# A channel-major residual stream, out and down projections with stationary weights, and weight parts in three slots at equal residues

## The chip, the cores and the metric

The kernel runs on one core of a Trainium2 chip. TensorE (PE) multiplies, VectorE (DVE) and ScalarE (ACT) work element by element, GpSimd (POOL) does a few small things, and SyncE (SP) issues the transfers of the weights. The metric is the device time of one execution in microseconds.

## The reference

One layer of a hybrid decoder on 256 tokens of 2048 channels, in float32. It needs these products, by far the largest part of the work:

```python
h = rmsnorm(x, g_mix);  proj = h @ w_in             # 2048 x 5200
x = x + concat([pool_out, attn_out]) @ w_out        # 2048 x 2048
u = rmsnorm(x, g_ffn) @ w_up                        # 2048 x 11264
uc = causal_conv3(u); gate, val = split(uc)
x = x + (silu(gate) * val) @ w_down                 # 5632 x 2048
x = x + (p @ w_ple_proj) * sigmoid(rmsnorm(x, g_ple) @ w_ple_gate)
return rmsnorm(x, g_final)
```

Between the first two lines stand trailing-mean pooling and a sparse attention whose indexer picks 64 keys for each query. The change does not touch either.

## The kernel before

**Products.** Every float32 operand is cut into a high part `hi` that TensorE takes in one pass (type float32r) and a low rest `lo`. A product is hi·hi + hi·lo + lo·hi. One *block* here is a 128x128 piece of a weight matrix, applied to all 256 tokens: 768 columns stream through the array for it, in one of two forms.

- `cm_matmul` (lines 121 to 127; "cm" for channel-major): the weight block is stationary. Line 125 streams the activations' hi and lo, 512 columns, past `hi`. Line 126 streams the activations' hi, 256 columns, past `lo`. A block is two matmuls and two weight loads, and the output has channels in the partitions.
- `tm_matmul` (lines 143 to 153; "tm" for token-major): a 128x128 tile of activations is stationary and 512 columns of weights stream past it. Lines 150, 151 and 152 are the three terms; four blocks take six matmuls of 512 columns. The output has tokens in the partitions.

Before the change w_qi, w_qk, w_u (together 512 blocks) and w_up (1408 blocks) are cm; w_first, w_out (256 blocks), w_down (704 blocks), w_pp and w_pg are tm.

**Units.** `unit` (lines 59 to 68) brings in 8 blocks of weights at a time: a DMA on SP's queue into one of four `raw` buffers, ACT copies it to `hi` (line 65), DVE subtracts to make `lo` (line 67). `hi` and `lo` come from two pools, `whi` and `wlo`, of three buffers each, 4416 bytes a buffer and partition, one behind the other. Units take these three slots in turn. In the built program slot s has `hi` at byte 91904 + 4416 s of each partition and `lo` at 105152 + 4416 s. The activations `hT`, 16 tiles of 2048 bytes (256 tokens hi, 256 tokens lo), stand at byte 36064; block i of a unit is 512 bytes further in the slot than block i - 1, and its tile of `hT` 2048 bytes further than the last.

**Residual.** `x` holds the stream with tokens in the partitions. `add_residual` (lines 169 to 174) adds 512 output columns of w_out or w_down to it and squares them on ACT. `to_hT` (lines 155 to 167) then transposes those four channel tiles on TensorE (line 162, eight transposes for 512 columns), and `split` writes hi and lo into `hT`. `rstd_col` and `rstd_rows` make the inverse root mean square as a column for each token and, with two small matmuls (line 117), as a row `rbc`. The first stage loads both x transposed (`xr`) and x itself.

**Order.** The instructions' order on each engine is set by a scheduler that simulates a timeline; each engine runs its queue strictly in order.

Of the kernel before, what the change touches and what calls it, by code (L numbers as in the profile page):

```python
# [10 lines left out]
F32 = mybir.dt.float32  # L11
# [24 lines left out]


# [7 lines left out]
def layer(ctx: ExitStack, tc: tile.TileContext, a: dict):  # L45
# [4 lines left out]
    cst = ctx.enter_context(tc.tile_pool(name="cst", bufs=1))  # L50
    wraw = ctx.enter_context(tc.tile_pool(name="wraw", bufs=4))
    whi = ctx.enter_context(tc.tile_pool(name="whi", bufs=3))
    wlo = ctx.enter_context(tc.tile_pool(name="wlo", bufs=3))
# [4 lines left out]

    def unit(src, n=1024, keep=None):

        size, bufs = (1024, 8) if keep else (UNIT, None)
# [3 lines left out]
        A.copy(hi[:, :n], raw[:, :n])  # L65
        lo = (keep or wlo).tile([P, size], F32R, name="lo", bufs=bufs)
        V.tensor_sub(lo[:, :n], raw[:, :n], hi[:, :n].bitcast(F32))  # L67
        return hi, lo
# [6 lines left out]
    x = cst.tile([P, 2, D], F32, name="x")  # L75
    hT = cst.tile([P, KT, 2 * S], F32R, name="hT")
    rbc = cst.tile([P, S], F32, name="rbc")
    mhalf = cst.tile([P, 2], F32, name="mhalf")
    G.memset(mhalf, -0.5)
    NU = 4  # L80
# [40 lines left out]
    def cm_matmul(ps, hi, lo, kts, first, last):  # L121

        for i, kt in enumerate(kts):
            w = slice(i * P, (i + 1) * P)
            T.matmul(ps, hi[:, w], hT[:, kt, :], start=first and i == 0, stop=False)  # L125
            T.matmul(ps[:, :S], lo[:, w], hT[:, kt, :S],  # L126
                     start=False, stop=last and i == len(kts) - 1)

    def cm_tile(src, c, ps=None):
        if ps is None:  # L130
            ps = acc.tile([P, 512], F32, name="pa")
        for h in range(2):
            hi, lo = unit(src[c][:, h * 1024:(h + 1) * 1024])
            cm_matmul(ps, hi, lo, range(8 * h, 8 * h + 8), h == 0, h == 1)
        return ps

    def cm_evict(dst, ps):
        b = tmp.tile([P, S], F32, name="eb", bufs=3)
# [16 lines left out]
    def to_hT(n, gcol):  # L155

        for kp in range(2):
            ps = aux.tile([P, 512], F32, name="ps")
            for j in range(2):
                kt = 4 * n + 2 * kp + j  # L160
                for t in range(2):
                    T.transpose(ps[:, j * S + t * P:j * S + (t + 1) * P],  # L162
                                x[:, t, kt * P:(kt + 1) * P], ident)
            for j in range(2):
                kt = 4 * n + 2 * kp + j
                split(hT[:, kt, :S], hT[:, kt, S:], ps[:, j * S:(j + 1) * S],
                      prm[:, gcol + kt:gcol + kt + 1])

    def add_residual(n, pss, ssq):
        for t in range(2):  # L170
            xs = x[:, t, n * 512:(n + 1) * 512]
            V.tensor_add(xs, pss[t], xs)
            sq = tmp.tile([P, 512], F32, name="sq")
            A.activation(sq, xs, AF.Square, accum_out=ssq[:, t, n:n + 1])

    def sum4(ssq):
        s = tmp.tile([P, 2], F32, name="s4")
        V.tensor_reduce(s, ssq, axis=AX.X, op=OP.add)
        return s

    ssq_f = cst.tile([P, 2, 4], F32, name="ssq_f")
    ssq_p = cst.tile([P, 2, 4], F32, name="ssq_p")


    with ExitStack() as c1:
        ar = c1.enter_context(tc.tile_pool(name="ar", bufs=1))
        catP = ar.tile([P, 8, 2 * S], F32R, name="catP")


        xr = [ar.tile([P, 8, S], F32, name="xr0", tag="tb"),  # L190
# [536 lines left out]
```

## Time and profile before

| | |
|---|---|
| device time, median of 3 (lowest, highest) | 1210.94 us (1210.93, 1210.98) |
| device time of the profiled execution | 1210.77 us |
| its span in the profile | 1209.0 us |
| PE busy | 1197.5 us, 99% |
| DVE, ACT busy | 817.0 us, 68%; 625.4 us, 52% |
| granted TensorE clock | 0.997 over the span |

[...] A float32 matmul that is not a transpose stands as two records, and a transpose or a float32r matmul as one.

### The profile page before, as it was taken

To read this page: it belongs to the slowest core of one execution; us is meant where nothing else is said; L and a number is where in the kernel's file an instruction comes from. 1 tells how busy PE (TensorE), PEld (TensorE's weight loads), DVE (VectorE), ACT (ScalarE), POOL (GpSimd) and SP (SyncE) were. 2 spreads that over 40 slices of the span, in tenths; PEclk is the share of its full clock that TensorE was granted. 3 is DMA by queue.
4 is the path that set the end of the run, shared out by engine and by line. 5 is a ranking of instruction groups with operands and counts; after the bars stand their busy time and mean duration, and the time that the engine had idled before them with its cause. 6 is when DMAs were issued, how large, how long until landed. Compare 5 with 4: busy or idle time off the path is not lost.

```text
span 1209.0 us, 16727 instructions
## 1 busy us (share of the span) xinstructions
PE 1197.5 (99%) x6332; PEld 1027.2 (85%) x6332; DVE 817.0 (68%) x1234; ACT 625.4 (52%) x951; POOL 8.5 (1%) x26
## 2 busy tenths in 40 slices
PE   9999999999999999999999999999999999999996
PEld 9988888888888888888888888888888888888886
DVE  6566866985557778777777877877545454545565
ACT  7455344555456555555555555555434343434453
POOL 0000000000000000000000000000000000000000
PEclk9999999999999999999999999999999999999998
DMA  9654665456665555555555555556666666666662
GB/s 359 221 184 158 231 201 179 141 161 187 187 186 180 189 190 191 190 188 191 188 188 191 189 193 189 188 191 186 190 190 187 187 183 190 185 187 220 189 213 85
DMA packets 66720, 230.46 MB, mean 191 GB/s; under 512 B 7792, under 2 KB 9464, under 8 KB 66512
## 3 DMA queue, kind: packets, MB, share of 16 engines
q1 hardware_dynamic: 63488, 223.88, 58.5%
q10 hardware_dynamic: 2144, 2.88, 0.7%
q0 software_dynamic: 1008, 2.64, 0.6%
q8 instruction: 49, 0.80, 0.3%
q14 instruction: 31, 0.25, 0.1%
HBM read 226.74 MB, written 3.68 MB: 191 GB/s over the span
## 4 chain that ended last, share of the span: by engine, by line
PE 98%; ACT 0%; DMA 0%; DVE 0%; SPq 0%; issue 0%; POOLq 0%; ACTq 0%
PE pa L125 36%; PE pa L126 19%; PE pa L152 12%; PE pa L151 12%; PE pa L150 12%; PE ps L151 1%; PE ps L152 1%; PE ps L150 1%; PE ps L162 1%; PE ps L290 1%; PE ps L467 0%; DMA raw<-in_w_first 0%; PE ps L377 0%; PE ps L291 0%; PE ps L125 0%; PE ps L428 0%
## 5 line engine op out<-in xcount | busy, mean ns | idle before, releaser
L67 DVE TENSOR_TENSOR lo<-raw,hi 128x1024 fp32r<-128x1024 f32 (+2 forms) x417 | 508.9, 1221 | 350.0 <-ACT hi L65 347.5
L65 ACT CAST hi<-raw 128x1024 fp32r<-128x1024 f32 (+2 forms) x417 | 435.9, 1046 | 534.3 <-issue 218.3
L125 PE MATMUL pa<-hT,hi 128*128 128x512 f32 x1904 | 665.8, 393 | 0.2 <-ACT hi L65 0.2
L126 PE MATMUL pa<-hT,lo 128*128 128x256 f32 x1904 | 534.6, 281 | 0.0
L125 PEld LDWEIGHTS pa<-hT,hi 128*128 128x128 f32 x1904 | 357.7, 188 | 81.4 <-issue 0.6
L126 PEld LDWEIGHTS pa<-hT,lo 128*128 128x128 f32 x1904 | 358.2, 188 | 0.2
L152 PE MATMUL pa<-hi,aT 128*128 128x512 f32 x352 | 138.5, 394 | 0.0
L151 PE MATMUL pa<-lo,aT 128*128 128x512 f32 x352 | 138.5, 393 | 0.0
L150 PE MATMUL pa<-hi,aT 128*128 128x512 f32 x352 | 126.0, 395 | 0.0
L151 PEld LDWEIGHTS pa<-lo,aT 128*128 128x128 f32 x352 | 66.1, 188 | 15.6
L152 PEld LDWEIGHTS pa<-hi,aT 128*128 128x128 f32 x352 | 66.1, 188 | 15.1
L150 PEld LDWEIGHTS pa<-hi,aT 128*128 128x128 f32 x352 | 66.1, 188 | 14.9
L151 PE MATMUL pa<-lo,hT 128*128 128x512 f32 (+2 forms) x208 | 74.8, 360 | 0.1
L152 PE MATMUL pa<-hi,hT 128*128 128x512 f32 (+2 forms) x208 | 74.8, 360 | 0.0
L150 PE MATMUL pa<-hi,hT 128*128 128x512 f32 (+2 forms) x208 | 65.1, 363 | 0.0
L534 ACT ACTIVATE cv<-ub,cnv 128x256 f32<-128x256 f32 x88 | 52.6, 598 | 1.1 <-DVE ub L141 1.0
L140 DVE TENSOR_TENSOR eb<-pa,eb 128x256 f32<-128x256 f32 x119 | 49.8, 418 | 0.0
L538 DVE SCALAR_TENSOR_TENSOR cv<-ub,cnv,cv 128x256 f32<-128x256 f32 x88 | 42.7, 485 | 3.0
L151 PEld LDWEIGHTS pa<-lo,hT 128*128 128x128 f32 x208 | 39.4, 190 | 5.4 <-DVE lo L67 0.4
L152 PEld LDWEIGHTS pa<-hi,hT 128*128 128x128 f32 x208 | 39.4, 189 | 4.9
L150 PEld LDWEIGHTS pa<-hi,hT 128*128 128x128 f32 x208 | 38.7, 191 | 5.7 <-ACT hi L65 0.5
L139 ACT COPY eb<-pa 128x256 f32<-128x256 f32 x119 | 43.5, 365 | 0.0
(174 smaller groups left out, 826.7 us busy)
## 6 DMA issues: line engine op xcount, KB each, us to landing
raw<-in_w_up SPq DMA_DIRECT2D x176, 512.0 KB, 4.7
raw<-in_w_down SPq DMA_DIRECT2D x88, 512.0 KB, 3.6
raw<-in_w_qk SPq DMA_DIRECT2D x32, 512.0 KB, 4.4
raw<-in_w_out SPq DMA_DIRECT2D x32, 512.0 KB, 3.7
raw<-in_w_pg SPq DMA_DIRECT2D x32, 512.0 KB, 4.4
raw<-in_w_first SPq DMA_DIRECT2D x15, 552.0 KB, 6.3
raw<-in_w_qi SPq DMA_DIRECT2D x16, 512.0 KB, 4.2
raw<-in_w_u SPq DMA_DIRECT2D x16, 512.0 KB, 4.2
```

The source lines that it names most:

```text
L65: A.copy(hi[:, :n], raw[:, :n])
L67: V.tensor_sub(lo[:, :n], raw[:, :n], hi[:, :n].bitcast(F32))
L125: T.matmul(ps, hi[:, w], hT[:, kt, :], start=first and i == 0, stop=False)
L126: T.matmul(ps[:, :S], lo[:, w], hT[:, kt, :S], start=False, stop=last and i == len(kts) - 1)
L139: A.copy(b, ps[:, S:])
L140: V.tensor_add(b, ps[:, :S], b)
L150: T.matmul(pss[t][:, :n], xh, hi[:, w], start=first and i == 0, stop=False)
L151: T.matmul(pss[t][:, :n], xh, lo[:, w], start=False, stop=False)
L152: T.matmul(pss[t][:, :n], xl, hi[:, w], start=False, stop=last and i == len(kts) - 1)
L162: T.transpose(ps[:, j * S + t * P:j * S + (t + 1) * P], x[:, t, kt * P:(kt + 1) * P], ident)
L534: A.activation(t, u[:, 2:], AF.Identity, bias=cnv[:, k + 3:k + 4], scale=cnv[:, k + 2:k + 3])
L538: V.scalar_tensor_tensor(t, u[:, :S], cnv[:, k:k + 1], t, op0=OP.mult, op1=OP.add)
```

## The change

`x` is replaced by `xt`, with channels in the partitions. w_out and w_down are stored by block and go through `cm_matmul`, one output tile of 128 channels at a time, w_out in pairs of tiles (`out_unit`). The new `add_residual` adds both halves of the PSUM tile on DVE, splits straight into `hT`, and after every second tile squares the pair on ACT and adds it to `ssa` on DVE. `rstd_tok` sums the squares over the channels with four float32 matmuls of two columns. The transposes move to the end: `to_rows` turns 512 channels of `xt` back to tokens for the last stage, while w_pg runs. The first stage no longer loads x, and w_qi's first tile moves ahead of `rstd_rows`.

The weights' `hi` and `lo` of a unit now share one tile `w` in one of three one-buffer pools `w0`, `w1`, `w2`. In the built program slot s is at byte 73760 + 12288 s, `lo` stands 5056 bytes behind `hi` (4416 in the wider units of the first stage). `hT` stays at 36064, and `catP` (130272), `catA` (146656) and `aT` (134368) get its residue 3296 modulo 4096.

```diff
+LOW, SLOT = 1264, 2304
+GAP_W, GAP_A, GAP_F = 144, 8, 176
...
+    gap.tile([P, GAP_W], F32, name="gap")
+    for i in range(3):
+        wsp.append(ctx.enter_context(tc.tile_pool(name=f"w{i}", bufs=1)))
+        mid.append(ctx.enter_context(tc.tile_pool(name=f"mid{i}", bufs=1)) if i < 2 else None)
+    rbc = mid[0].tile([P, S], F32, name="rbc")
+    ssa = mid[0].tile([P, 2 * S], F32, name="ssa")
...
-        hi = (keep or whi).tile([P, size], F32R, name="hi", bufs=bufs)
-        lo = (keep or wlo).tile([P, size], F32R, name="lo", bufs=bufs)
+            w = wsp[n_units % 3].tile([P, SLOT], F32R, name="w")
+            n_units += 1
+            l0 = LOW if n <= 1024 else UNIT
+            hi, lo = w[:, :n], w[:, l0:l0 + n]
...
-    x = cst.tile([P, 2, D], F32, name="x")
+    xt = cst.tile([P, KT, S], F32, name="xt")
...
+    def add_residual(c, ps, gcol):
+        xs = xt[:, c, :]
+        V.tensor_add(xs, ps[:, :S], xs)
+        V.tensor_add(xs, ps[:, S:], xs)
+        split(hT[:, c, :S], hT[:, c, S:], xs, prm[:, gcol + c:gcol + c + 1])
+        if c % 2:
+            square(c // 2)
...
+            A.activation(sq, pair, AF.Square)
+            V.tensor_add(ssa, ssa, sq)
...
+    def rstd_tok(name):
+        ps = aux.tile([P, 512], F32, name="ps")
+        for t in range(2):
+            for h in range(2):
+                T.matmul(ps[:, 2 * t:2 * t + 2], ssa[:, h * S + t * P:h * S + (t + 1) * P], ones2,
+                         start=h == 0, stop=h == 1)
+        return rstd_col(ps[:, 0:4:2], name)
...
-                in_order(nc.sync.dma_start(x[:, :, cs], a["x"][:, :, cs]))
...
+        for c0 in range(0, KT, 2):
+            ps2 = [acc.tile([P, 512], F32, name="pa") for _ in range(2)]
+            for h in range(2):
+                for e in range(2):
+                    out_unit(c0 + e, ps2[e], h)
+                    if c0 + h + e == 0:
+                        pool_map(*done.pop())
+            for e in range(2):
+                add_residual(c0 + e, ps2[e], C_GFFN)
...
+        for c in range(KT):
+            ps = acc.tile([P, 512], F32, name="pa")
+            for k0 in range(0, NF, 8):
+                k1 = min(k0 + 8, NF)
+                hi, lo = unit(a["w_down"][c][:, k0 * P:k1 * P], (k1 - k0) * P)
+                cm_matmul(ps, hi, lo, tiles(aT, range(k0, k1)), k0 == 0, k1 == NF)
+            add_residual(c, ps, C_GPLE)
...
+        def to_rows(n):
+            for t in range(2):
+                ps = aux.tile([P, 512], F32, name="ps")
+                for j in range(4):
+                    T.transpose(ps[:, j * P:(j + 1) * P], xt[:, 4 * n + j, t * P:(t + 1) * P],
+                                ident)
+                A.copy(gx[:, t, n * 512:(n + 1) * 512], ps)
```

In the changed kernel `cm_matmul` is on lines 145 and 146, `unit`'s two halves on 85 and 86, the ones matmuls on 200, `rstd_rows` on 137 and the last transposes on 604.

PE before, where 512 columns of w_out end and the next begin (`catP` are activations, `ident` the identity, x the residual):

```order
L150 MATMUL pa<-hi,catP 128x512
L151 MATMUL pa<-lo,catP 128x512
L152 MATMUL pa<-hi,catP 128x512
L162 MATMUL ps<-ident,x 128x128 x2
L150 MATMUL pa<-hi,catP 128x512
L162 MATMUL ps<-ident,x 128x128 x6
L151 MATMUL pa<-lo,catP 128x512
L152 MATMUL pa<-hi,catP 128x512
```

PE in the changed kernel, inside w_out, where one unit ends on `catA` and the next begins on `catP`:

```order
L145 MATMUL pa<-catA,w 128x512
L146 MATMUL pa<-catA,w 128x256
L145 MATMUL pa<-catA,w 128x512
L146 MATMUL pa<-catA,w 128x256
L145 MATMUL pa<-catP,w 128x512
L146 MATMUL pa<-catP,w 128x256
L145 MATMUL pa<-catP,w 128x512
L146 MATMUL pa<-catP,w 128x256
```

The six 512-column matmuls of four blocks have become four pairs of 512 and 256 columns, and nothing stands between one output tile and the next.

PE before, at the end of the first stage (`r_mix` is the first inverse root mean square, `hT` the activations):

```order
L150 MATMUL ps<-hi,hT 128x368
L151 MATMUL ps<-lo,hT 128x368
L152 MATMUL ps<-hi,hT 128x368
L117 MATMUL ps<-ident,r_mix 128x128 x2
L125 MATMUL ps<-hT,hi 128x512
L126 MATMUL ps<-hT,lo 128x256
```

PE in the changed kernel, at the same place, from the end of w_qi's first unit to the end of its second; between the two pieces stand 12 more of the matmuls of lines 145 and 146:

```order
L145 MATMUL ps<-hT,w 128x512
L146 MATMUL ps<-hT,w 128x256
L200 MATMUL ps<-ones_101,ssa 128x2 x4
L145 MATMUL ps<-hT,w 128x512
L146 MATMUL ps<-hT,w 128x256
...
L145 MATMUL ps<-hT,w 128x512
L146 MATMUL ps<-hT,w 128x256
L137 MATMUL ps<-ident,r_mix 128x128 x2
L145 MATMUL pa<-hT,w 128x512
L146 MATMUL pa<-hT,w 128x256
```

The four ones matmuls are new, and the two of `rstd_rows` now come one unit behind them instead of long behind the sums.

DVE in the changed kernel between the same two places (`ms` is the mean square, w the weights' low part):

```order
L86 TENSOR_TENSOR w<-raw,w 128x1024 x3
L120 TENSOR_SCALAR ms<-ps 128x2
L86 TENSOR_TENSOR w<-raw,w 128x1024
L128 TENSOR_TENSOR r_602<-r_600 128x2
L129 SCALAR_TENSOR_TENSOR r_602<-r_602,ms 128x2
L131 SCALAR_TENSOR_TENSOR r_mix<-r_602,r_600 128x2
```

DVE before, with the same chain in the middle of the first stage:

```order
L178 TENSOR_REDUCE s_568<-ssq_102 128x2
L100 TENSOR_SCALAR ms<-s_568 128x2
L108 TENSOR_TENSOR r_574<-r_572 128x2
L109 SCALAR_TENSOR_TENSOR r_574<-r_574,ms 128x2
L67 TENSOR_TENSOR lo<-raw,hi 128x1104
L111 SCALAR_TENSOR_TENSOR r_mix<-r_574,r_572 128x2
```

The chain from the mean square to `r_mix` has a subtraction of weights inside it in both, and its first link now waits for TensorE.

## Rows read from the trace of the kernel before

**Rows 1.** The page: busy time of each engine, and the chain that ended last.

```profile
PE 1197.5 (99%) x6332; PEld 1027.2 (85%) x6332; DVE 817.0 (68%) x1234; ACT 625.4 (52%) x951; POOL 8.5 (1%) x26
...
PE 98%; ACT 0%; DMA 0%; DVE 0%; SPq 0%; issue 0%; POOLq 0%; ACTq 0%
```

**Rows 2.** The waits of PE, all of them: waiter, releaser, us, times, longest.

```profile
PE ps L207 <- POOL rbc L82: 1.1, 1, 1.1
PE pa L125 <- ACT hi L65: 0.2, 1, 0.2
```

**Rows 3.** Timeline, PE, w_up: the first matmul of five units running (start, us, line).

```profile
405.37 0.39 PE L125 MATMUL pa<-hT,hi 128*128 128x512 f32 x1
...
408.12 0.40 PE L125 MATMUL pa<-hT,hi 128*128 128x512 f32 x1
...
410.90 0.40 PE L125 MATMUL pa<-hT,hi 128*128 128x512 f32 x1
...
413.72 0.39 PE L125 MATMUL pa<-hT,hi 128*128 128x512 f32 x1
...
416.47 0.40 PE L125 MATMUL pa<-hT,hi 128*128 128x512 f32 x1
```

**Rows 4.** Stretches: busy us (x count) of PE, PEld, DVE, ACT, POOL; clock, DMA share, GB/s.

```profile
0.00:50.00 50.00, 48.79 (x267) 47.30 (x268) 28.00 (x38) 31.97 (x52) 1.54 (x9) 1.00 0.87 316
384.00:848.00 464.00, 464.00 (x2670) 407.50 (x2669) 370.46 (x589) 265.92 (x420) 0.00 (x0) 1.00 0.59 190
918.00:978.00 60.00, 60.00 (x261) 48.72 (x260) 28.93 (x28) 25.26 (x29) 0.00 (x0) 1.00 0.64 187
1121.00:1142.00 21.00, 21.00 (x92) 17.00 (x91) 12.76 (x14) 11.83 (x15) 0.00 (x0) 1.00 0.59 182
```

**Rows 5.** Timeline, PE, w_down: from one group of transposes to the next.

```profile
916.39 0.38 PE L162 MATMUL ps<-ident,x 128*128 128x128 f32 x2
...
916.84 0.82 PE L162 MATMUL ps<-ident,x 128*128 128x128 f32 x6
917.41 0.48 PE L151 MATMUL pa<-lo,aT 128*128 128x512 f32 x1
917.73 0.39 PE L152 MATMUL pa<-hi,aT 128*128 128x512 f32 x1
917.96 0.39 PE L150 MATMUL pa<-hi,aT 128*128 128x512 f32 x1
...
978.10 0.39 PE L152 MATMUL pa<-hi,aT 128*128 128x512 f32 x1
```

**Rows 6.** Timeline, PE: small float32 matmuls (two records each) and the matmul behind.

```profile
79.16 0.49 PE L290 MATMUL ps<-kx,qx 64*128 64x128 f32 x2
79.57 0.39 PE L291 MATMUL ps<-kr,qr 128*128 128x256 f32 x1
...
369.10 0.60 PE L117 MATMUL ps<-ident,r_ffn 128*128 128x128 f32 x4
369.46 0.36 PE L126 MATMUL pa<-hT,lo 128*128 128x256 f32 x1
369.66 0.40 PE L125 MATMUL pa<-hT,hi 128*128 128x512 f32 x1
```

**Rows 7.** Timeline: links of the chain to `r_mix`, and a unit's ACT and DVE work.

```profile
36.52 0.17 DVE L100 TENSOR_SCALAR ms<-s 128x2 f32<-128x2 f32 x1
36.84 0.70 POOL L106 TENSOR_TENSOR r<-ms,mhalf 128x2 f32<-128x2 f32 x1 [35.47 <-DVE ms L100]
37.57 0.16 DVE L108 TENSOR_TENSOR r<-r 128x2 f32<-128x2 f32 x1 [0.88 <-POOL r L106]
...
49.07 1.05 ACT L65 CAST hi<-raw 128x1024 fp32r<-128x1024 f32 x1 [1.89 <-PE ps L152]
50.15 1.23 DVE L67 TENSOR_TENSOR lo<-raw,hi 128x1024 fp32r<-128x1024 f32 x1 [1.63 <-ACT hi L65]
```

**Rows 8.** The page, costliest groups: DVE's 256-column sum out of PSUM (busy, mean ns).

```profile
L140 DVE TENSOR_TENSOR eb<-pa,eb 128x256 f32<-128x256 f32 x119 | 49.8, 418 | 0.0
```

More of the change, by code (lines that the diff above doesn't have):

```diff
@@ L119, in rstd_rows, with cm_matmul, tiles, cm_tile @@
         V.tensor_copy(rbc, ps[:, :S])
-    def cm_matmul(ps, hi, lo, kts, first, last):
-        for i, kt in enumerate(kts):
+    def cm_matmul(ps, hi, lo, acts, first, last):
+        for i, act in enumerate(acts):
             w = slice(i * P, (i + 1) * P)
[L125 to L131, printed above, removed]
+            T.matmul(ps, hi[:, w], act, start=first and i == 0, stop=False)
+            T.matmul(ps[:, :S], lo[:, w], act[:, :S],
+                     start=False, stop=last and i == len(acts) - 1)
+    def tiles(act, kts):
+        return [act[:, kt, :] for kt in kts]
+    def cm_tile(src, c):
+        ps = acc.tile([P, 512], F32, name="pa")
         for h in range(2):
             hi, lo = unit(src[c][:, h * 1024:(h + 1) * 1024])
-            cm_matmul(ps, hi, lo, range(8 * h, 8 * h + 8), h == 0, h == 1)
+            cm_matmul(ps, hi, lo, tiles(hT, range(8 * h, 8 * h + 8)), h == 0, h == 1)
         return ps
     def cm_evict(dst, ps):
-        b = tmp.tile([P, S], F32, name="eb", bufs=3)
+        b = mid[1].tile([P, S], F32, name="eb", bufs=3)
         A.copy(b, ps[:, S:])
@@ L153, in tm_matmul @@
                          stop=last and i == len(kts) - 1)
[L155 to L167, printed above, removed]
@@ L232, in layer @@
         in_order(nc.sync.dma_start(cnv, a["conv"]))
-        r_mix = rstd_col(sum4(ssq0), "r_mix")
+        ps_q = aux.tile([P, 512], F32, name="ps")
+        for h in range(2):
+            hi, lo = unit(a["w_qi"][0][:, h * 1024:(h + 1) * 1024])
+            cm_matmul(ps_q, hi, lo, tiles(hT, range(8 * h, 8 * h + 8)), h == 0, h == 1)
+            if h == 0:
+                r_mix = rstd_tok("r_mix")
         rstd_rows(r_mix)
-        kd = ar.tile([P, 2, 2, 64], F32, name="kd")
-        wx = ar.tile([P, 2, IH], F32, name="wx")
         v = ar.tile([P, 2, NH * P], F32, name="v")
@@ L492, in layer, with out_unit @@
         attend(6, pts[6])
-        def out_units(n, pss, gs, first, last):
-            for i, g in enumerate(gs):
-                hi, lo = unit(a["w_out"][n][:, g * 1024:(g + 1) * 1024])
-                act, k0 = (catP, 2 * g) if g < 4 else (catA, 2 * g - 8)
-                tm_matmul(pss, hi, lo, act, (k0, k0 + 1), first and i == 0,
-                          last and i == len(gs) - 1)
-        def out_done(n, pss):
-            add_residual(n, pss, ssq_f)
-            to_hT(n, C_GFFN)
-        for n in range(4):
-            pss = [acc.tile([P, 512], F32, name="pa") for _ in range(2)]
-            out_units(n, pss, (3, 2, 1), True, False)
-            if n == 0:
-                pool_map(*done.pop())
-            out_units(n, pss, (4, 5, 6, 7, 0), False, True)
-            out_done(n, pss)
+        cats = tiles(catP, range(2, 8)) + tiles(catA, range(8)) + tiles(catP, range(2))
+        def out_unit(c, ps, h):
+            hi, lo = unit(a["w_out"][c][:, h * 1024:(h + 1) * 1024])
+            cm_matmul(ps, hi, lo, cats[8 * h:8 * h + 8], h == 0, h == 1)
+        for c0 in range(0, KT, 2):
+            ps2 = [acc.tile([P, 512], F32, name="pa") for _ in range(2)]
+            for h in range(2):
+                for e in range(2):
[4 more added lines that the diff above has]
+                add_residual(c0 + e, ps2[e], C_GFFN)
     pin = ctx.enter_context(tc.tile_pool(name="pin", bufs=1))
@@ L708 @@
         "rel_bias": i["rel_bias"],
-        "w_out": _tm(i["w_out"][0]),
+        "w_out": _cm(i["w_out"][0].reshape(KT, P, D)[np.r_[2:16, 0:2]].reshape(D, D)),
         "w_up": _cm(i["w_up"][0])[order],
-        "w_down": _tm(i["w_down"][0]),
+        "w_down": _cm(i["w_down"][0]),
         "w_pg": _tm(i["w_ple_gate"][0]),
```

109 lines of the change are left out of this document (51 added, 58 removed).

## The prediction

> **What bounds the kernel now.** I read the page's busy times and its chain first. PE is busy for 1197.5 of 1209.0 us and 98% of the chain that ended last is PE, while DVE and ACT are at 68% and 52% [rows 1]. Then the waits: in the whole span PE waits 1.1 us for POOL at the start and 0.2 us for ACT once [rows 2]. So no transfer and no other engine sets the time. A busy PE is not yet a fast one, though, so the next thing to read is how far the starts of matmuls lie apart. [...]
>
> The view that matters most is the timeline of w_up. Five units running are shown by their first matmul; each unit is the same work, 8 blocks in 16 matmuls. They take 408.12 - 405.37 = 2.75, 2.78, 2.82 and then 2.75 us again [rows 3]. The reader is to see that equal units have three prices and that the price comes back at the fourth unit. Only one thing comes back after three: the slot. Counting the records of lines 125 and 126 against the built program's order says which: 2.78 us is slot 0, 2.75 slot 1, 2.82 slot 2. Per block that is 347.5, 343.75 and 352.5 ns; three units make 8.35 us for 24 blocks, 347.9 on the mean. The long stretch agrees: 2670 matmuls, or 1335 blocks, in 464 us are 347.6 ns [rows 4].
>
> So the *place* of the weights has a price. While one matmul streams its activations, PEld loads the weights of the next, and both read the same partitions. I take as measure the distance from the activations being streamed to the weights being loaded, modulo 1024, worked out from the addresses given above. For slot 1 it runs 800, 352, 288, 864 through two blocks; slot 0 lies 320 bytes lower and slot 2 320 higher. In the changed kernel it runs 768, 320, 256, 832: slot 1's, 32 bytes lower. It is so in all three slots, since 12288 is a multiple of 4096, and in w_out and w_down too, since catP, catA and aT share hT's residue.
>
> **The change part by part**, against the profiled execution's span of 1209.0 us.
>
> *The new price of a block.* The changed kernel is a tenth of the way from slot 1 to slot 0. Reading straight between them gives 343.75 + (347.5 - 343.75)/10 = 344.1, and I take **344 ns**, because slot 1 is by far the nearest row. Nothing says that the price runs straight between slots, and no row of cm lies closer than 32 bytes. The bounds are 341.5 below (as far under slot 1 as a little more than half of its distance to slot 0) and slot 2's 352.5 above.
>
> [...]
>
> *Blocks that stay cm.* w_qi, w_qk, w_u and w_up are 512 + 1408 = 1920 blocks: 1920 x (347.9 - 344) = **7.5 us saved**. All of it is on the path, since PE is the path.
>
> *Blocks that go from tm to cm.* In w_down the third matmul after a group of transposes starts at 917.96, and the last before the next group, 260 matmuls later (261 touch the stretch from 918 to 978 us [rows 4]), at 978.10 [rows 5]: 231.3 ns each, and 1.5 of them make a block, 347.0. That is the mean price of cm to within 1 ns, so the form alone gives nothing: the same 768 columns go through. With the new price 704 + 256 blocks save 960 x (347.0 - 344) = **2.9 us**. I take w_out at w_down's price.
>
> *Transposes.* A group of eight with the two matmuls among and behind it takes from 916.39 to 917.73, 1.34 us, of which the two matmuls are 0.46: 0.88 us a group [rows 5]. Eight groups (four in w_out, four in w_down) go, 7.0 us. Four groups come back in w_pg, 3.5 us, as 4 and 4 or 3 and 5 transposes, interrupting as often as before. **3.5 us saved.**
>
> *Ones matmuls.* Three times four small float32 matmuls are new, 24 records. The nearest row is line 117: four records and the late start behind them push line 126's successor to 369.66, 0.56 us less one matmul of 0.12, or 0.11 a record [rows 6]. Line 290's take 0.41 us for two [rows 6], 0.2 a record. I take 0.11, **2.6 us lost**, with 1.7 (0.07 a record, as for the first two transposes of [rows 5], 0.14 us) and 5.0 as bounds.
>
> *Waits that could appear.* At the end of the first stage the ones matmuls stand one unit, 2.75 us, ahead of `rstd_rows`. Behind them run 0.17 us on DVE, 0.70 on POOL and three links of 0.16 on DVE [rows 7], 1.35 in all; but in DVE's queue a subtraction for a later unit stands among the links, and it waits for ACT's copy into the slot that the first unit frees. Copy, subtraction and last links are 1.05 + 1.23 + 0.48 = 2.76 us [rows 7], and the copy can start 0.9 us before the ones matmuls end. I cost it at nothing; the cover is w_qi's second unit, and without it PE would stand still for up to 1.4 us, and all later units behind it. At w_up there are 30 matmuls, 5.2 us, for the same chain, and in w_pg PE does not wait for it.
>
> *Work that goes to DVE and ACT.* For two tiles of w_out, four units or 11 us, DVE has four subtractions of 1.23 us [rows 7], six 256-column operations of 0.42 [rows 8] and one sum of 512, put at twice that: 8.3 us, 75%. In w_up it is at 370.46 of 464, 80% [rows 4], and PE has no wait there. w_down has fewer tiles for its units and is easier, ACT easier still. So nothing, hidden by the units' 2.75 us on PE; only if DVE had gone over 100% would each further us be paid in full.
>
> *Loads of x* (2 MB fewer in the first stage): the DMA engines are 87% busy there, but PE lacks 1.2 of 50 us [rows 4], which is the wait for POOL [rows 2]. Nothing. *w_pg's* tm matmuls read from new places as well; the trace has no cm row for them, and I bound them by the spread of [rows 3], 1.3% of some 100 us, both ways.
>
> The sum is -7.5 - 2.9 - 3.5 + 2.6 = -11.3 us: a span of 1197.7. Outside the span lie 1210.77 - 1209.0 = 1.8 us, and the median of the runs is 0.2 above the profiled execution: **1199.5 us**.
>
> **The rivals.**
>
> *The place is worth nothing* (the distance is not the cause, or the mean price returns): 344 becomes 347.9. The first term is 0, the second 960 x 0.9 = 0.9 lost, the rest stays at -0.9: **1211 us**. For it speaks that the prices were never tried apart; against it that they come back unit by unit. [...]
>
> *All units at the dear slot's price* (slower): if the 32 bytes matter more than the 320 between slots, for instance because hT and the weights now begin at the same residue modulo 64, which they did not in cm before, every block could cost slot 2's 352.5. Then 1920 x 4.6 + 960 x 5.5 - 900 ns = 13.2 us lost, **1224 us**. Three slots at one distance leave no cheap slot to offset a dear one; it decides from a price of 348.2 on. Against it: in w_down before, both begin at a multiple of 64, and its price is 347.0, not dear [rows 5].
>
> *Better than slot 1*: 341.5 a block, 2880 x 2.5 = 7.2 us more, and cheap ones matmuls: **1191.5 us**.
>
> **How the numbers follow.** The forecast (1194 to 1206) gets 0.64, the better price 0.08, no effect 0.13, the dear price 0.15. The range goes from 1191 to 1214: it takes in the no-effect case and the low bound and leaves out most of the dear case. Each ns of a block's price is 2.9 us, so it is no narrower. A measurement of this kernel can tell 0.2%, 2.4 us, from no change. Faster than that: 0.64 + 0.08 + 0.03 of the no-effect case = 0.75; within it 0.08; slower 0.15 + 0.02 = 0.17.
>
> **What would show it.** Right: in w_up all three units of a cycle take 2.75 us, the same in w_out and w_down; no transposes there; PE's waits stay under 2 us; PE about 98% of the chain. Wrong: units at 2.78 or 2.82 us (the price), units that still differ (the distance is not the measure), a PE wait at lines 200 or 137 (the chain), or DVE releasing PE in w_out (the load).

## The result, and the profile after

The changed kernel takes 1196.12 us, the median of 4 runs (1195.62 to 1197.66), against 1210.96 for the kernel before, measured beside it: a ratio of 0.9879, 95% interval 0.9862 to 0.9897. The profiled execution took 1197.66 us, with a span of 1195.9. One run of those below, 1224.34 us among the four with w_out's first group widened, is slow and enters no median and no ratio.

The page after, busy times and chain, as [rows 1] of before:

```profile
PE 1181.3 (99%) x6804; PEld 1039.2 (87%) x6804; DVE 853.7 (71%) x1308; ACT 641.9 (54%) x943; POOL 9.1 (1%) x27
...
PE 97%; issue 1%; DVE 1%; DMA 0%; ACT 0%; SPq 0%; POOLq 0%; ACTq 0%
```

PE is still the bound, and its busy time fell by 16.2 us. The waits of PE, all of them, as [rows 2] (waiter, releaser, us in total, times, longest):

```profile
PE pa L172 <- ACT w L85: 1.4, 2, 0.7
PE ps L224 <- POOL rbc L102: 1.2, 1, 1.2
PE ps L482 <- ACT plr L110: 0.6, 1, 0.6
PE pa L145 <- DVE catP L114: 0.6, 1, 0.6
PE pa L145 <- ACT w L85: 0.4, 1, 0.4
```

They grew from 1.3 us to 4.2. Two are in the first stage (line 172), the last three where w_out begins. The timeline of PE in w_up, every eighth block, as [rows 3] (start, us, line):

```profile
404.65 0.39 PE L145 MATMUL pa<-hT,w 128*128 128x512 f32 x1
...
407.37 0.39 PE L145 MATMUL pa<-hT,w 128*128 128x512 f32 x1
...
410.09 0.39 PE L145 MATMUL pa<-hT,w 128*128 128x512 f32 x1
...
412.81 0.39 PE L145 MATMUL pa<-hT,w 128*128 128x512 f32 x1
```

Eight blocks take 2.72 us each time, in all three slots; before, it was 2.78, 2.75 and 2.82. The stretches, columns as in [rows 4]:

```profile
0.00:50.00 50.00, 47.33 (x264) 45.42 (x265) 31.37 (x40) 30.48 (x44) 0.87 (x9) 1.00 0.80 276
384.00:848.00 464.00, 464.00 (x2731) 411.01 (x2730) 385.60 (x600) 284.96 (x427) 0.00 (x0) 1.00 0.59 193
918.00:978.00 60.00, 60.00 (x355) 53.09 (x354) 32.53 (x39) 26.21 (x30) 0.00 (x0) 1.00 0.66 193
1121.00:1142.00 21.00, 21.00 (x93) 16.94 (x92) 12.69 (x14) 9.96 (x14) 0.00 (x0) 1.00 0.60 178
```

In the 464 us of w_up stand 2731 matmuls where 2670 stood, 339.8 ns a block for 347.6, at the same granted clock of 1.00. The last row is w_pg's token-major work, with two transposes among its 93 matmuls; by the starts, 768 columns take 348.5 ns there for 348.3 before.

The record of a 512-column matmul in w_up is 0.39 us long and the next matmul's begins 0.22 or 0.23 us behind its start, so prices are read from the starts. Where the 13.1 us of span went, from the first matmul of each stage to that of the next (us; block prices are the distance from one 512-column matmul to the next, averaged over a stage's blocks of 0.4 us or less; for token-major blocks, one and a half times the distance between two 512-column matmuls):

| stage | before | after | difference | price of a block |
|---|---|---|---|---|
| w_first | 54.9 | 55.4 | +0.5 | token-major |
| w_qi, w_qk, w_u, attention | 209.4 | 211.3 | +1.9 | 349.3 to 346.1 |
| w_out | 94.5 | 94.1 | -0.4 | 348.1 to 349.3 |
| w_up | 491.6 | 480.3 | -11.3 | 347.9 to 340.1 |
| w_down | 246.9 | 239.4 | -7.5 | 347.0 to 340.0 |
| w_pp, w_pg, end of PE | 101.6 | 105.3 | +3.7 | token-major |

Two things cross the borders of these stages. Of the eight groups of transposes before, three stand in w_out (2.6 us) and three in w_down; the last of w_out's runs inside w_up, and the last of w_down's inside w_pp. And eight matmuls of the attention (lines 428 and 430 before, 443 and 445 after), 1.2 us, stood behind w_out's first matmul before and stand ahead of it after, so 1.2 us of the second row's +1.9 belong to the third.

So the gain is w_up and w_down, and w_out, which lost three groups of transposes, gave nothing.

### The profile page after: what moved, and what is told of

The parts are those of the page before. It is cut to its first block, busy times and chain, and to the rows that moved or that the text cites. A ratio compares the mean times of both kernels' runs of the same rounds, so it can differ in the third digit from the quotient of the medians.

```text
span 1195.9 us, 17848 instructions
## 1 busy us (share of the span) xinstructions
PE 1181.3 (99%) x6804; PEld 1039.2 (87%) x6804; DVE 853.7 (71%) x1308; ACT 641.9 (54%) x943; POOL 9.1 (1%) x27
## 4 chain that ended last, share of the span: by engine, by line
PE 97%; issue 1%; DVE 1%; DMA 0%; ACT 0%; SPq 0%; POOLq 0%; ACTq 0%
PE pa L145 54%; PE pa L146 27%; PE pa L173 3%; PE pa L174 3%; PE pa L172 3%; PE ps L174 1%; PE ps L173 1%; PE ps L172 1%; PE ps L308 1%; DMA raw<-in_w_first 0%; PE ps L392 0%; PE ps L309 0%; PE ps L482 0%; PE ps L145 0%; PE ps L604 0%
## 5 line engine op out<-in xcount | busy, mean ns | idle before, releaser
L86 DVE TENSOR_TENSOR w<-raw,w 128x1024 fp32r<-128x1024 f32 (+3 forms) x420 | 503.0, 1199 | 229.9 <-ACT w L85 222.9
L145 PE MATMUL pa<-hT,w 128*128 128x512 f32 x1904 | 652.3, 390 | 0.0
L85 ACT CAST w<-raw 128x1024 fp32r<-128x1024 f32 (+3 forms) x420 | 433.0, 1032 | 350.4 <-PE pa L146 250.2
L146 PE MATMUL pa<-hT,w 128*128 128x256 f32 x1904 | 528.9, 278 | 0.0
L145 PEld LDWEIGHTS pa<-hT,w 128*128 128x128 f32 x1904 | 357.4, 188 | 74.9 <-issue 0.6
L146 PEld LDWEIGHTS pa<-hT,w 128*128 128x128 f32 x1904 | 358.0, 188 | 0.3
L145 PE MATMUL pa<-aT,w 128*128 128x512 f32 x704 | 239.4, 389 | 0.0
L146 PE MATMUL pa<-aT,w 128*128 128x256 f32 x704 | 194.3, 276 | 0.0
L145 PEld LDWEIGHTS pa<-aT,w 128*128 128x128 f32 x704 | 132.2, 188 | 27.6
L146 PEld LDWEIGHTS pa<-aT,w 128*128 128x128 f32 x704 | 132.2, 188 | 0.0
L173 PE MATMUL pa<-w,hT 128*128 128x512 f32 (+2 forms) x178 | 65.1, 366 | 0.1
L174 PE MATMUL pa<-w,hT 128*128 128x512 f32 (+2 forms) x178 | 64.9, 365 | 0.0
L172 PE MATMUL pa<-w,hT 128*128 128x512 f32 (+2 forms) x178 | 58.5, 368 | 1.4 <-ACT w L85 1.4
L145 PE MATMUL pa<-catP,w 128*128 128x512 f32 x128 | 46.3, 397 | 0.7 <-DVE catP L114 0.6
L172 PEld LDWEIGHTS pa<-w,hT 128*128 128x128 f32 x178 | 32.7, 188 | 6.3 <-ACT w L85 2.0
```

Source lines behind the costliest of these rows:

```text
L85: A.copy(hi, raw[:, :n])
L86: V.tensor_sub(lo, raw[:, :n], hi.bitcast(F32))
L145: T.matmul(ps, hi[:, w], act, start=first and i == 0, stop=False)
L146: T.matmul(ps[:, :S], lo[:, w], act[:, :S], start=False, stop=last and i == len(acts) - 1)
L172: T.matmul(pss[t][:, :n], xh, hi[:, w], start=first and i == 0, stop=False)
L173: T.matmul(pss[t][:, :n], xh, lo[:, w], start=False, stop=False)
```

## The experiments

The theory was that the place of the weights, measured as the distance from the activations that stream to the weights that are loaded meanwhile, sets the price of a block. The rivals were that the place is worth nothing and the gain comes from the channel-major form, or that something else in the change (the slots 12288 bytes apart, the residue modulo 4096) does it.

### The changed kernel once more

No edit. After the first profile w_out stood at 350 ns a block and w_up and w_down at 340, at one and the same distance, so the question was whether both prices are that place's.

> The changed kernel unaltered, for a second profile. In the first profile a block costs 340.0 ns in w_up and w_down and 350 ns in w_out, at the same distance between weights and activations. Theory A (one distance has two paces, and PE keeps the one that it fell into until something interrupts the stream): w_out may show 340 or 350 this time, and each early stretch between small matmuls one of two paces, so runs scatter by up to 2.6 us (256 blocks x 10 ns); 1195.5 to 1197.7 us. Theory B (350 belongs to catP and catA as operands): w_out is at 350 again, the early stretches are as before, and the scatter has another source.

1196.53 us, ratio 0.9883 (0.9869 to 0.9898). w_up and w_down stood at 340.0 again, but w_out, by the count of PE's matmuls from 310 to 350 us, did not. First the changed kernel's first profile, then this run:

```profile
310.00:350.00 40.00, 40.00 (x230) 35.20 (x229) 28.02 (x40) 19.24 (x25) 0.00 (x0) 1.00 0.58 188
```

```profile
310.00:350.00 40.00, 40.00 (x237) 35.39 (x236) 28.96 (x42) 20.33 (x26) 0.00 (x0) 1.00 0.60 193
```

230 matmuls are 348 ns a block, 237 are 338 (one more or less at the ends of the stretch is 1.5 ns); by the starts it is 350 and 340. So 350 is not the price of `catP` and `catA` as operands. The same program at the same addresses ran w_out at two paces, after a wait that differed by 6 ns between the runs (532 and 538 ns from one start to the next). The first profile shows both within 12 us of w_up. Timeline of PE there:

```profile
366.46 0.39 PE L145 MATMUL pa<-hT,w 128*128 128x512 f32 x1
...
367.16 0.39 PE L145 MATMUL pa<-hT,w 128*128 128x512 f32 x1
...
367.86 0.39 PE L145 MATMUL pa<-hT,w 128*128 128x512 f32 x1
...
368.80 0.95 PE L200 MATMUL ps<-ones,ssa 128*128 128x2 f32 x8
369.61 0.36 PE L146 MATMUL pa<-hT,w 128*128 128x256 f32 x1
...
371.19 0.39 PE L145 MATMUL pa<-hT,w 128*128 128x512 f32 x1
...
371.87 0.39 PE L145 MATMUL pa<-hT,w 128*128 128x512 f32 x1
...
372.55 0.39 PE L145 MATMUL pa<-hT,w 128*128 128x512 f32 x1
```

Rows two blocks apart: 0.70 us ahead of the ones matmuls, 0.68 behind them. Here four small matmuls stand between the two paces. No wait and no small matmul is needed, though: in w_out of both runs the pace turned where one block's 256-column matmul stands behind another's, at 291 us of the first profile from 340 to 350 and at the same matmul of this run from 353 to 340. The first profile there:

```profile
289.73 0.39 PE L145 MATMUL pa<-catA,w 128*128 128x512 f32 x1
...
290.41 0.39 PE L145 MATMUL pa<-catP,w 128*128 128x512 f32 x1
...
290.98 0.28 PE L146 MATMUL pa<-catP,w 128*128 128x256 f32 x1
291.09 0.28 PE L146 MATMUL pa<-catA,w 128*128 128x256 f32 x1
291.21 0.40 PE L145 MATMUL pa<-catA,w 128*128 128x512 f32 x1
...
291.91 0.40 PE L145 MATMUL pa<-catA,w 128*128 128x512 f32 x1
```

Where hi and lo alternated without such a break, the pace held, from 375 us to the end of w_down in both runs.

### Channel-major alone

```diff
-            w = wsp[n_units % 3].tile([P, SLOT], F32R, name="w")
-            l0 = LOW if n <= 1024 else UNIT
-            hi, lo = w[:, :n], w[:, l0:l0 + n]
+            hi = whi.tile([P, UNIT], F32R, name="hi")[:, :n]
+            lo = wlo.tile([P, UNIT], F32R, name="lo")[:, :n]
...
-GAP_W, GAP_A, GAP_F = 144, 8, 176
+GAP_W, GAP_A, GAP_F = 72, 368, 536
```

> The changed kernel, but hi and lo again come from two pools of three contiguous 4416-byte buffers, at the very distances from hT that they had before the change; catP, catA and aT keep hT's residue. So this is the channel-major part of the change alone. Theory A (the distance sets the price): units in w_up take 2.75, 2.78 and 2.82 us in turn again, 347.9 ns a block on the mean, in w_down too; 2112 blocks x 7.9 ns = 16.7 us lost, about 1212 us, no faster than before. Rival (the weights-stationary form and the missing transposes made the gain, the place nothing): 340 ns a block stays and the time is 1196 us. Half way (1204) would mean that the slots' equality counts beside the distance.

1211.81 us, ratio 1.0008 (0.9999 to 1.0018): all of the gain is gone, though the transposes of w_out and w_down are gone too. Its stretches of w_up and w_down:

```profile
384.00:832.00 448.00, 448.00 (x2579) 393.42 (x2578) 356.38 (x564) 256.33 (x404) 0.00 (x0) 1.00 0.60 189
872.00:1072.00 200.00, 200.00 (x1153) 175.77 (x1152) 105.70 (x124) 85.74 (x99) 0.00 (x0) 1.00 0.65 190
```

347.4 and 346.9 ns a block. By slot, units take 2.772, 2.755 and 2.820 us in w_down, as in w_up and as before the change [rows 3]; so the prices go with the place of the weights and not with the activations' buffer (`hT` or `aT`, at one residue here) or the stage.

### The place alone

The kernel before, with three gaps and wider rows that give its three slots the distances of the changed kernel modulo 256 bytes; its squares get one buffer in place of two, to make room.

```diff
+    g0 = ctx.enter_context(tc.tile_pool(name="g0", bufs=1)).tile([P, 8], F32, name="g0")
     whi = ctx.enter_context(tc.tile_pool(name="whi", bufs=3))
+    g1 = ctx.enter_context(tc.tile_pool(name="g1", bufs=1)).tile([P, 48], F32, name="g1")
     wlo = ctx.enter_context(tc.tile_pool(name="wlo", bufs=3))
+    g2 = ctx.enter_context(tc.tile_pool(name="g2", bufs=1)).tile([P, 40], F32, name="g2")
...
-        size, bufs = (1024, 8) if keep else (UNIT, None)
+        size, bufs = (1024, 8) if keep else (1152, None)
```

> The kernel before, token-major out and down projections and all, with only the weight pools moved: three gaps and rows of 4608 in place of 4416 bytes put all three slots at the changed kernel's distance from hT modulo 256 bytes. Theory A: w_up's 1408 blocks fall from 347.9 to 340 ns and save 11 us, the blocks of w_qi, w_qk and w_u stand at 340 or 350 as entered and give 0 to 2 us, the token-major stages are unknown within 4 us: 1200 us (1195 to 1204). Rival (the period is 4096 bytes, or the slots must be 12288 apart): two or three different unit prices stay, 1208 to 1214. Rival (the gain needs channel-major projections): 1211.

1200.04 us, ratio 0.9914 (0.9897 to 0.9930), with token-major projections and all. Its stretch of w_up:

```profile
384.00:832.00 448.00, 448.00 (x2637) 396.96 (x2636) 364.93 (x579) 262.41 (x412) 0.00 (x0) 1.00 0.59 194
```

2637 matmuls are 339.8 ns a block, the changed kernel's own price, from slots 4608 bytes apart at other residues modulo 4096. Together with the last run this is a table of two by two: neither edit 1211, channel-major alone 1212, place alone 1200, both 1196. Channel-major is worth 4 us at the good place and nothing at the old one. Some 2 of the 4 come from the token-major side: w_down's stage, still token-major, took 249.0 us here for 246.9 before (350.0 ns a block for 347.0), so the new place is dearer for that form.

### The dear place

hi moves up by 96 bytes in its slot and lo down by 160, which is the same modulo 256: both come to the distance of slot 2 before.

```diff
-LOW, SLOT = 1264, 2304
+LOW, SLOT = 1200, 2304
...
-            hi, lo = w[:, :n], w[:, l0:l0 + n]
+            hi, lo = w[:, 24:24 + n], w[:, 24 + l0:24 + l0 + n]
```

> The changed kernel with both weight parts moved up 96 bytes inside their slots, which is the distance of slot 2 in the kernel before; the same instructions in the same order. Theory A: every channel-major unit costs about 2.82 us, 2368 blocks of w_out, w_up and w_down go from 340.6 to 353 ns and cost 29 us, the early stretches 1 to 2 us more: 1227 us (1223 to 1231), 1.3% slower than the kernel before, so that the same change at another place would have been a loss. Rival (the slots' spacing, not the distance, made the gain): 1196.

1230.14 us, ratio 1.0163 (1.0148 to 1.0178): the same instructions in the same order, 34 us slower than the changed kernel and slower than the kernel before. In w_up:

```profile
384.00:832.00 448.00, 448.00 (x2538) 387.33 (x2537) 363.11 (x559) 266.35 (x401) 0.00 (x0) 1.00 0.55 187
```

353.0 ns a block, and by the starts 353.3 to 353.5 in the early stretches, w_out, w_up and w_down alike. Against the changed kernel's first profile the price explains 1408 x 13.2 + 704 x 13.3 + 256 x 4.2 + 512 x 7.2 ns = 32.7 us of the 34. Most of the rest, 1.4 us, is five blocks of w_out at 640 ns each: TensorE had stood still twice (1032 and 994 ns from start to start, where w_out begins), and behind that the granted clock fell, to 0.54 over the 3.5 us around these blocks (from 299 to 317 us it is 1.00 again):

```profile
273.50:277.00 3.50, 3.50 (x12) 2.98 (x13) 0.45 (x1) 0.00 (x0) 0.00 (x0) 0.54 0.41 142
```

The changed kernel's first profile has the same two waits and no fall of the clock behind them (1.00 from 264 to 288 us).

### Is it 256 bytes?

hi moves up by 256 bytes in its slot and lo down by 256.

```diff
-LOW, SLOT = 1264, 2304
+LOW, SLOT = 1136, 2304
...
-            hi, lo = w[:, :n], w[:, l0:l0 + n]
+            hi, lo = w[:, 64:64 + n], w[:, 64 + l0:64 + l0 + n]
```

> The changed kernel with hi moved up and lo moved down by 256 bytes inside the slots; the same instructions in the same order. Theory A with a period of 256 bytes: nothing changes, 1196.3 us (1194.5 to 1198), w_up and w_down at 340 ns a block or, at the worst, one of them at the other pace of 350 (+7 or +14 us). Rival (the residue modulo 4096 or 1024 matters, as the change words it): block prices between 343 and 353 that differ from both paces, 1204 to 1228.

1197.21 us, ratio 0.9890 (0.9876 to 0.9905), with the same paces as in the first profile: w_up 340.1, w_down 340.0, w_out 348.9. One residue modulo 4096 is not needed; modulo 256 is enough.

### Two maps of TensorE alone

The first runs 16 blocks at each of 32 distances, the layer's offset between hi and lo kept, and four times each behind a small float32 matmul of 2, 64, 128 or 200 columns.

```python
for sh in range(0, 1024, 32):
    l0 = (768 + sh) % 1024 // 4;  h0 = l0 + 1040
    for n in (2, 64, 128, 200):
        T.matmul(ps[:, :n], ident, xt[:, 0, :n], start=True, stop=True)
        # then 16 blocks as in cm_matmul, lo from w[:, l0:], hi from w[:, h0:]
```

> TensorE alone: line 84 and 85 stream 16 blocks of cm matmuls from one fixed set of activations and weights, behind one small float32 matmul of 2, 64, 128 or 200 columns, for 32 distances between activations and weights in steps of 32 bytes; nothing else runs, and the layer's result is left out. Shift 0 is the changed kernel's distance, 32 slot 1's, 352 slot 2's and 704 slot 0's of the kernel before. Theory A: the price of a block depends on the shift: about 340 or 350 at 0, 343.75 at 32, 352.5 at 352, 347.5 at 704, and the same again at no other place than the period; where a shift has two paces, the four entries show both. Rival (the price in the layer comes from DVE, ACT or DMA touching the same memory): without them all shifts cost the same, and no entry differs.

The price (over the last ten blocks) came back every 256 bytes, entry by entry and to 0.1 ns, but for the very first stream: 353.3 or 350.0 at the changed kernel's distance, by the entry, then in steps of 32 bytes 343.3 or 352.0, 346.7, 353.3, 346.7, 353.3, 346.7 to 351.6, and 346.7 or 350.0. The three slots before lie at 224 (slot 0), 32 (slot 1) and 96 (slot 2) of it, and their units' 346.5, 344.4 and 352.5 ns in the layer agree to 1.1 ns. With nothing but TensorE at work the prices differ as they do in the layer, so they do not come from DVE, ACT or DMA touching the same memory. The pace of 340 did not appear in this map. A typical stretch of it, at 353 ns (starts 0.70 or 0.71 apart over two blocks):

```profile
99.76 0.39 PE L84 MATMUL pa<-act,w 128*128 128x512 f32 x1
...
100.47 0.39 PE L84 MATMUL pa<-act,w 128*128 128x512 f32 x1
```

The second moves lo and hi independently, 8 x 8 places. The small matmuls meant to separate the two entries were put elsewhere by the scheduler, so most streams ran through 16 or 32 blocks, and the map tells nothing of entries.

> This kernel leaves the whole layer out: TensorE alone runs 16 channel-major blocks (a 512-column and a 256-column matmul each) for each of 64 pairs of distances, lo and hi moved by 0, 32, ... 224 bytes independently, twice: entered by a small fp32 matmul ahead of block 0, and by one between hi and lo of block 0. The changed kernel's place is lo 0, hi 64; the slots of the kernel before lie on the diagonal hi = lo + 64. Theory A (two distances set the price, each for the matmul that streams while that part is loaded): the gap of the 512-column matmul follows the place of lo and that of the 256-column matmul the place of hi, so the 64 prices are sums of 8 + 8 numbers to about 2 ns; the diagonal repeats 340 or 350 at lo 0, 343 or 352 at lo 32, 353 at lo 96, 347 at lo 224; and 340 appears at lo 0, hi 64 for at least one of the two entries. Rival (the price belongs to the step from lo to hi, or to the pool): prices change along a row and a column together, with no sum to be made. Rival (distance is not it): all 64 within 2 ns.

Price of a block in ns, over 10 blocks of the first stream of each pair; rows are the place of lo, columns that of hi, modulo 256 from the activations. The changed kernel is at lo 0, hi 64:

```
lo\hi    0     32     64     96    128    160    192    224
  0   346.6  351.4  340.0  346.7  352.0  349.3  340.0  344.5
 32   346.7  353.3  351.2  352.0  352.7  346.6  346.7  348.5
 64   346.6  346.7  353.3  348.0  347.3  348.7  346.7  346.7
 96   351.2  349.9  353.3  346.6  351.6  353.3  348.9  346.9
128   350.0  353.9  350.0  351.5  350.6  346.7  346.6  348.4
160   346.7  350.7  353.3  353.3  350.6  350.0  349.3  353.3
192   346.7  350.7  353.3  349.1  353.3  353.3  353.5  353.4
224   353.4  346.6  350.3  350.0  346.7  346.7  349.0  346.7
```

Two pairs of 64 stand at 340.0 and nothing is lower. The changed kernel's place is thus the best of this grid, or one of two. Timeline of PE at that pair, two blocks in 0.68 us:

```profile
43.98 0.39 PE L86 MATMUL pa<-act,w 128*128 128x512 f32 x1
44.21 0.28 PE L89 MATMUL pa<-act,w 128*128 128x256 f32 x1
44.32 0.39 PE L86 MATMUL pa<-act,w 128*128 128x512 f32 x1
44.55 0.28 PE L89 MATMUL pa<-act,w 128*128 128x256 f32 x1
44.66 0.39 PE L86 MATMUL pa<-act,w 128*128 128x512 f32 x1
```

My expectation that the price is a sum of one number for lo and one for hi fell: 340.0 + 346.6 (lo 0 with hi 64, lo 64 with hi 0) should equal 346.6 + 353.3 (lo 0 with hi 0, lo 64 with hi 64), and is 13 ns less. The best sum of one number for each row and one for each column misses single pairs by up to 7.5 ns. So the two places act together, as far as a map can say in which a pair may also have a second pace.

One thing no run tried: in the layer's runs and in both maps the activations that stream past these weights stand at one residue (3296 modulo 4096), and only the weights moved. Whether the distance between the two counts, or the weights' own address modulo 256, is open, and "distance" is one reading of these runs.

### The other pair

hi alone moved up by 128 bytes, to lo 0, hi 192.

```diff
+            h0 = 32 if n <= 1024 else 0
-            hi, lo = w[:, :n], w[:, l0:l0 + n]
+            hi, lo = w[:, h0:h0 + n], w[:, l0:l0 + n]
```

> The changed kernel with hi alone moved up 128 bytes in its slots (lo stays where it is): the pair lo 0, hi 192 of the pair map, the only other one that stood at 340.0 ns a block there. The same instructions in the same order. If the map holds for the layer, w_up and w_down stay at 340; if this pair has no second pace, the early stretches (480 blocks at 346 to 347 ns in the changed kernel) and w_out (256 at 349) come down to 340 too and the kernel takes 1191 us (1189 to 1194). If it has two paces like the pair of the changed kernel, 1196.5 (1194 to 1199). If the map does not carry over to the layer, block prices of 345 to 355 and 1203 to 1230 us.

1192.90 us, ratio 0.9852 (0.9838 to 0.9867). The map holds in the layer: w_up and w_down stay at 340.0, w_out comes to 340.4 and the early stretches to 341.7. w_out:

```profile
286.00:356.00 70.00, 70.00 (x414) 62.04 (x414) 51.31 (x73) 35.56 (x45) 0.00 (x0) 1.00 0.62 201
```

The changed kernel's first profile has 403 matmuls in this stretch. Ahead of it, behind the first two waits of w_out, the granted clock of this profiled execution fell for five blocks at 640 ns, to 0.51 over the 3.5 us around them, as at the dear place:

```profile
267.00:270.50 3.50, 3.50 (x13) 2.91 (x13) 0.03 (x1) 0.00 (x0) 0.00 (x0) 0.51 0.34 117
```

That is 1.5 us. The four runs fit it: two at a mean granted clock of 0.996 took 1193.6 and 1193.9 us, two at 0.997 took 1191.9 and 1192.2. This pair has a second pace as well (the last run below, with w_out in another order, ran at 350 from 264 to 269 us, until a small matmul stood between a hi and a lo), but its streams fell into the faster one nearly everywhere.

### The waits at the start of w_out

In the first profile PE's starts in w_out lie 1031, 993, 943 and 532 ns apart at four places where 115 to 235 is usual: some 2.7 us. Timelines there, of PE, DVE and ACT in turn (in brackets the idle time before, and what ended it):

```profile
268.21 0.39 PE L482 MATMUL ps<-plr,w 128*128 128x256 f32 x1 [0.64 <-ACT plr L110]
268.46 0.39 PE L146 MATMUL pa<-catP,w 128*128 128x256 f32 x1
269.45 0.50 PE L145 MATMUL pa<-catP,w 128*128 128x512 f32 x1 [0.60 <-DVE catP L114]
...
285.23 0.50 PE L145 MATMUL pa<-catA,w 128*128 128x512 f32 x1 [0.44 <-ACT w L85]
```

```profile
278.52 0.47 DVE L114 SCALAR_TENSOR_TENSOR catP<-ps,prm,catP 128x256 fp32r<-128x256 f32 x1
```

```profile
277.05 0.47 ACT L113 ACTIVATE catP<-ps,prm 128x256 fp32r<-128x256 f32 x1
283.18 2.94 ACT L85 CAST w<-raw 128x1024 fp32r<-128x1024 f32 x3 [5.66 <-issue]
```

The first is a pooling product that waits for its input from ACT, the second waits for rows of `catP` that the pooling makes just then. The last two are another kind. The two blocks of each second unit that need the last pooled rows are put behind (those rows are ready at 279.0, the blocks run from 282.36 on), so three units stay open, no weight slot is free, and ACT's three copies all wait until 283.18 (read from the order; the profile names no releaser). The edit makes the first group four tiles wide and puts the last pooling product one unit later:

```diff
-        for c0 in range(0, KT, 2):
+        for c0, n in [(0, 4)] + [(c, 2) for c in range(4, KT, 2)]:
...
-                    if c0 + h + e == 0:
+                    if c0 + h == 0 and e == 1:
```

> The changed kernel with w_out's first group made of four channel tiles in place of two, and the last pooling product put behind its second unit in place of its first. In the changed kernel TensorE waits there four times (1031, 993, 943 and 532 ns from one matmul's start to the next, where 115 to 230 is usual), since the pooled rows come late and their blocks hold all three weight slots. If these waits are that order's doing, they go and 2.5 us with them: 1193.7 us (1192 to 1196), less 2.4 more if w_out falls into the pace of 340. If they are the DMA's (raw weights late for another reason), waits of the same size stay: 1196.5.

1195.90 us, ratio 0.9878 (0.9858 to 0.9897), less than expected: the waits of the second kind went, but two (935 and 1020 ns) stayed, both for `catP` and a little earlier, w_out ran at 350, and against the changed kernel's own medians of 1196.1 and 1196.5 the gain is within the spread of runs.

### Both, and the rows of w_out in another order

> The two edits before together: hi at the pair lo 0, hi 192, and w_out's first group of four channel tiles. If w_out's waits cost what the profile of the last run says (two of about 1 us are left of four), 1.5 us come off the 1192.9 us of the pair alone: 1191.5 (1190.3 to 1192.9), all block prices at 340. If the waits only moved, 1192.9 again.

The first of the two runs has the last two edits together and no other. 1190.82 us, ratio 0.9835 (0.9821 to 0.9848): 2.1 us better than the other pair alone, with no fall of the clock in its profile; some of the 2.1 may be that fall, which by their clocks two of the four runs of the pair alone had. The two remaining waits were for pooled group 1, so the last version takes its rows later:

```diff
-        cats = tiles(catP, range(2, 8)) + tiles(catA, range(8)) + tiles(catP, range(2))
+        cats = (tiles(catP, range(4, 8)) + tiles(catA, range(6)) + tiles(catP, range(2, 4))
+                + tiles(catA, range(6, 8)) + tiles(catP, range(2)))
...
-        "w_out": _cm(i["w_out"][0].reshape(KT, P, D)[np.r_[2:16, 0:2]].reshape(D, D)),
+        "w_out": _cm(i["w_out"][0].reshape(KT, P, D)[np.r_[4:14, 2:4, 14:16, 0:2]].reshape(D, D)),
```

> The same with the rows of w_out taken in another order (pooled groups 3 and 2 first, then six heads, then pooled group 1, the last two heads and pooled group 0), so that the first units need no row that is made just before them. If the last two waits (about 1 us each ahead of w_out's first blocks) came from rows of pooled group 1 being late, they go: 1190 us (1189 to 1191.5). If another wait takes their place, as late as the run before: 1191.5.

1189.45 us, median of 5, ratio 0.9826 (0.9812 to 0.9839): 21 us faster than the kernel before and about 7 faster than the changed one. All that PE still waits for:

```profile
PE pa L173 <- ACT w L86: 1.3, 1, 1.3
PE ps L225 <- POOL rbc L103: 1.2, 1, 1.2
```

## Why the prediction was right, point by point

**The mechanism** held. PE sets the time, and the place of the weights sets PE's pace: the place alone gives 11 us and the channel-major form alone none. Moving the weights by 96 and 160 bytes between two otherwise equal programs made 34 us. It is not the clock: the granted clock is 1.00 in w_up before, after and at the dear place alike. Nor is it the other engines: in the maps the prices differ by up to 13.9 ns (340.0 to 353.9) with none of them at work. What happens inside TensorE was not seen.

**The price of a block** was the term that was mis-sized, and the reason given for it was wrong. 344 ns came from reading straight between two slots. Over all 2880 blocks the price after is (512 x 346.1 + 256 x 349.3 + 1408 x 340.1 + 704 x 340.0) / 2880 = 342.0 ns, inside the bounds of 341.5 and 352.5, but the price does not run straight between places: 32 bytes move it by up to 12 ns, the period is 256 bytes and not 1024, and at the new place no stream runs at 344. It runs at 340, at 350 or, in a few early streams, at 353. That the price came out below 344 was luck: the straight line held nothing that told the new place from the 346 to 353 that most places of the pair map cost.

| term | predicted | measured in the first profile |
|---|---|---|
| blocks that stay channel-major | -7.5 | -12.6: w_up 1408 x 7.8 ns = 11.0, early stretches 512 x 3.2 = 1.6 |
| blocks from token-major | -2.9 | -4.6: w_down 704 x 7.0 = 4.9; w_out, nearly all at 350, lost 0.3 |
| transposes | -3.5 | -3.5: eight groups go, 7.0; w_pg takes up four of 0.87 |
| ones matmuls | +2.6 | +2.4: 0.8 us for each of three groups (368.80 to 369.61 above) |
| waits | 0 | +3.2: w_out 2.7, w_first 0.5 |
| small matmuls of the attention, and `rstd_rows` | not named | +1.2: 0.9 and 0.3 |

These come to -13.9 where the span fell by 13.1; the 0.8 us between are late starts in the early stretches and in w_out that no row names. The prediction's price of a token-major block in w_down, 347.0, is confirmed. That the total came within 3.4 us of the forecast was in part luck: the blocks gave 6.8 us more than predicted, and 4.4 us of waits and small matmuls that it had at nothing took most of that back. Two slips in its arithmetic are small: its own terms add to 1199.6 and not 1199.5, and break even at a price of 347.9 and not 348.2.

**The other steps.** The chain to `r_mix`, costed at nothing, was nothing: no wait stands at lines 200 or 137. DVE's load was hidden, as said: it releases PE once in w_out, for `catP`. By the letter that was one of the signs of being wrong, but it is a late operand and not DVE's load. The cost of 0.11 us for a record of the ones matmuls, taken from line 117's, was right (0.10). What the prediction did not look at was the order at the seam between pooling and w_out. In the kernel before that seam had no wait worth naming, since the pooled rows were needed three units later; the change asks for them after one. A stretch that is rewritten has to be read for its own waits, not only for the price of its matmuls. The 0.9 us of small matmuls in the attention stretch (those of lines 308, 309 and 445 cost 0.3 to 0.4 us more each in all, measured to the next start, than their counterparts before) were not followed further.

**The rivals.** "Place worth nothing" is what channel-major alone gave, 1211.8 against the 1211 worked out for it. "All units dear" is what 96 bytes more, modulo 256, would have given: 1230 against 1224. It was one placement away, and its reason, a shared residue modulo 64, was not the cause: the changed kernel shares it and the dear place does not. "Better than slot 1" came nearest in its cause: w_up and w_down lie under its 341.5, and the early stretches, w_out and the waits kept the time from its 1191.5.

**What would show it:** units of one price in all slots, yes, of 2.72 us and not 2.75; the same in w_down, yes; in w_out only in some executions; PE's waits under 2 us, no, 4.2; PE about 98% of the chain, 97%.

## What to carry to other kernels

When equal units of work take different times in turn, find what turns with them, and hold its place still before anything else is changed. A price that depends on an address is not to be interpolated: run a small map of the engine alone over the places, and then choose. Where an edit changes form and place at once, build the table of two by two; here it shows that the large rewrite paid, 4 us, only beside the small one.

## What the runs showed that was not expected

- The price of a float32r block of 512 and 256 columns on PE runs from 340.0 to 353.9 ns with the place of the weights, modulo 256 bytes from the activations (which were not moved themselves). Where the granted clock fell (0.54 and 0.51 over the two stretches), a block took 640 ns at the dear place and at the good pair alike, which cost 353 and 340 ns at 1.00. Whether any place costs less than 340 at 1.00, no run shows.
- One place can have several paces: 340, 350 and, in some early streams and the first map, 353 at the changed kernel's. Which one a stream takes changes where it starts again after a wait or a small matmul, or where two 256-column matmuls follow each other, and a difference of 6 ns in the wait went along with a different pace. What decides it was not found; the map meant to separate the entries could not.
- Part of a kernel's own spread goes with the granted clock. Behind the two waits at the start of w_out it was 1.00 in the changed kernel's first profile, and 0.54 and 0.51 over 3.5 us at the dear place and at the other pair, where five blocks cost 1.4 and 1.5 us more; the other pair's runs took 1193.6 and 1193.9 us at a mean clock of 0.996, 1191.9 and 1192.2 at 0.997. The paces may be another part (argued, not shown): the changed program took 1194.8 to 1197.9 us, and w_out's 256 blocks at the one or the other pace are 2.6 us.
